# Hybrid RWKV-7 / sparse-attention block: two of a joint FFN tile's seven products made ahead, and the second merge begun with RWKV's part

## The chip, the cores and the metric

The kernel runs on one core of a Trainium2 chip. The metric is device time in microseconds (us), the median of a few runs. Beside the times there is one profiled execution, whose span is counted from its first to its last recorded instruction. Engines are named as in the profile: PE is TensorE, PEld its weight load, DVE VectorE, ACT ScalarE, POOL GpSimd, SP the engine that issues most DMAs.

## The reference

One decoder layer over 1024 tokens with model width 1024, in fp32:

```python
u = rmsnorm(x, norm1_g);  proj = u @ w_in
y_a = rwkv7_mix(token_shift(p_rwkv), ...)              # 8 heads of 64, a scan over tokens
y_b = dsa_attention(rope(q), rope(k), v, ...)          # 8 heads, 256 keys chosen per query
merged = sigmoid(p_ga) * (y_a @ w_o_rwkv) + sigmoid(p_gb) * (y_b @ w_o_att)
h = x + merged @ w_out
z_gate, z_up = split(rmsnorm(h, norm2_g) @ w_ffn_in)   # 2 x 2816 columns
h = h + (silu(z_gate) * z_up) @ w_ffn_out
out = rmsnorm(h, normf_g)
```

The change touches the second half of attention, the second merge, the FFN and the last norm.

## The kernel before

**Layout.** Activations lie transposed: 128 channels on the partitions, 512 tokens (one of two halves) along the free axis. A product over 1024 channels is eight blocks. Every fp32 product is made of three reduced-precision ones: an operand is split into a high part (an ACT copy into the fp32r type, line 114) and a low part (a DVE subtraction, line 115), and `mm3` multiplies high by high, high by low (lines 144 and 145) and low by high (149). A 128-column weight tile against one half thus costs 24 matmuls of 512 columns. `mm3_last` (159) and `mm3_late` (1232, 1236) are the same products in an order that needs the last block, or the low part of the activations, late.

**Weights.** `weights` loads a raw tile into one of three `wst` buffers (125) and splits it into `whi`/`wlo`, of which there are two pairs. PSUM has three accumulators `acc` and five `mix`; `tmp` is a ring of four scratch tiles, 512 wide.

**Order.** PE's order is written out by hand: it runs in program order. The other engines' orders are set by the framework's scheduler, with some blocks given a high priority, and each engine and DMA queue then serves in order. Work of the first half is laid into the gaps of other stages by generators: `fill` is a queue of them, each of which yields after a few matmuls with their number, and `pump(n)` advances the queue until n of them are spent. `run` exhausts a generator; `run_over` exhausts one, and spends the negative numbers that it yields on `fill`.

**The stages around the change.** During the RWKV scan of the second half, `fill` holds the last gate tile, the first half's merge and the first half's `early` FFN. Then `attend(1)` runs 16 units (four head pairs by four query blocks): scores, a masked minimum on DVE (1062), an exponent on ACT (1065), transposes (1074), values (1084), and at a head pair's end `close`, which sends the sums through DRAM and scales the output. Its yields say how much fill goes in between. After it the rest of the fill runs.

`merge(1)` loads y_a and y_b, splits them, makes both parts of `w_o` per 128 output columns under the two gates, then `w_out`, adds x, writes h to DRAM, makes the unnormalised z = h times the norm's gain, split into `zhi`/`zlo`, and sums the squares. The norm's factor per token (a row) is applied later, in `swiglu`, to the FFN's products. It is made in `columns` (sums over channels on PE, a power on POOL), then `spread` (259, 274).

The FFN has 22 tiles of 128 gate and 128 up columns. `early(half)` does tiles 0 to 7 and their output (`ffn_out`), then 8 to 11 and theirs, for one half. `joint` does tiles 12 to 21 for both halves: the 2 x 2 block product of [gate, up] weights (each cut into two channel halves) by the two token halves is made of seven products instead of eight, in the manner of Strassen and Winograd. Its combined activations `t1`, `t2`, `t3`, `t4` come from `combined` (POOL subtractions, then splits), the combined weights from POOL sums in `joint_in` (1404). `ffn_out` adds its result to h in DRAM. The last two tiles' output is made in `finish_out`, which keeps h in SBUF, and makes the last norm in three passes: the first half, then 256 and 256 tokens of the second.

## Time and profile before

| | us |
|---|---|
| median of 3 runs | 1789.42 |
| lowest, highest | 1788.69, 1790.65 |
| the profiled execution | 1789.51 |
| its span | 1787.7 |
| mean granted clock of PE | 0.982 |

A row of a group reads: line, engine, operation, output<-inputs by the program's names, shape, count; busy us, mean ns; idle time of the engine before them and what ended it. In a list in order of time, a bracket holds the idle time just before the instruction and what released it.

### The profile page before, as it was taken

The numbers are of one execution on the slowest core, as the hardware profiler recorded it, in microseconds if no ns is written. First come the engines' busy times: TensorE is split into PE (matmuls) and PEld (weight loads), VectorE is DVE, ScalarE is ACT, GpSimd is POOL, SyncE is SP. The second block draws the span as 40 slices with busy tenths as digits, with TensorE's granted clock in tenths as the row PEclk, the third lists the DMA queues.
The fourth block names the chain that finished last, engine by engine and source line by source line (L and its number), as shares of the span: only waits on it lengthen the run. The fifth ranks groups of instructions, "written<-read, shape, count | busy, mean of one in ns | idle before, by whom it ended". The sixth has DMA issues, their size and how long they took to land. (4 is left out here: it accounts for less than half of the span.)

```text
span 1787.7 us, 26739 instructions
## 1 busy us (share of the span) xinstructions
PE 1707.8 (96%) x9952; PEld 1397.8 (78%) x9952; DVE 1191.6 (67%) x2249; ACT 834.7 (47%) x1592; POOL 222.8 (12%) x203
## 2 busy tenths in 40 slices
PE   8999999999999989999999999798799989999996
PEld 6888888788877767887888887586688878888785
DVE  6789899865576468758857655456753558567467
ACT  6365997543444877544333547333331323123132
POOL 0000000010021110000002111005700032031030
PEclk9999999999999999999999999898999999999998
DMA  5542334444375336733345674463235351541633
GB/s 205 175 138 83 107 104 149 144 127 146 122 208 160 105 109 204 218 112 99 113 125 159 192 204 130 161 195 98 68 113 170 92 159 54 159 142 41 208 130 128
DMA packets 139874, 248.20 MB, mean 139 GB/s; under 512 B 37680, under 2 KB 61936, under 8 KB 139616
## 3 DMA queue, kind: packets, MB, share of 16 engines
q1 hardware_dynamic: 116384, 172.66, 31.0%
q10 hardware_dynamic: 15552, 47.75, 8.5%
q0 software_dynamic: 7808, 26.09, 5.4%
q8 instruction: 78, 1.28, 0.3%
q14 instruction: 52, 0.43, 0.1%
HBM read 185.06 MB, written 61.39 MB: 138 GB/s over the span
## 5 line engine op out<-in xcount | busy, mean ns | idle before, releaser
L115 DVE TENSOR_TENSOR wlo<-wst,whi 128x1024 fp32r<-128x1024 f32 (+1 forms) x209 | 240.5, 1152 | 179.3 <-PE acc L149 78.6
L114 ACT ACTIVATE whi<-wst 128x1024 fp32r<-128x1024 f32 (+1 forms) x209 | 202.4, 970 | 269.6 <-PE acc L145 167.1
L144 PE MATMUL acc<-zhi,whi 128*128 128x512 f32 x352 | 142.2, 404 | 12.6 <-ACT whi L114 5.7
L144 PE MATMUL acc<-u1hi,whi 128*128 128x512 f32 x352 | 140.9, 400 | 0.0
L145 PE MATMUL acc<-zlo,whi 128*128 128x512 f32 x352 | 140.1, 398 | 0.0
L145 PE MATMUL acc<-u1lo,whi 128*128 128x512 f32 x352 | 138.8, 394 | 0.0
L144 PE MATMUL acc<-u0hi,whi 128*128 128x512 f32 (+1 forms) x352 | 135.3, 387 | 1.8 <-DVE tmp L343 1.8
L145 PE MATMUL acc<-u0lo,whi 128*128 128x512 f32 (+1 forms) x352 | 133.8, 383 | 0.0
L144 PE MATMUL acc<-fhi,whi 128*128 128x512 f32 x256 | 101.8, 398 | 1.9 <-ACT whi L114 1.0
L145 PE MATMUL acc<-flo,whi 128*128 128x512 f32 x256 | 100.1, 391 | 0.0
L144 PEld LDWEIGHTS acc<-zhi,whi 128*128 128x128 f32 x352 | 68.0, 193 | 29.4 <-ACT whi L114 6.7
L149 PE MATMUL acc<-u1hi,wlo 128*128 128x512 f32 x352 | 90.3, 395 | 0.0
L149 PE MATMUL acc<-zhi,wlo 128*128 128x512 f32 x352 | 88.4, 391 | 0.0
L149 PE MATMUL acc<-u0hi,wlo 128*128 128x512 f32 (+1 forms) x352 | 86.6, 385 | 0.0
L144 PEld LDWEIGHTS acc<-u1hi,whi 128*128 128x128 f32 x352 | 67.4, 191 | 14.8 <-DVE tmp L334 0.5
L145 PEld LDWEIGHTS acc<-zlo,whi 128*128 128x128 f32 x352 | 68.1, 193 | 13.7
L144 PEld LDWEIGHTS acc<-u0hi,whi 128*128 128x128 f32 x352 | 66.2, 188 | 15.2 <-ACT stg L114 2.2
L145 PEld LDWEIGHTS acc<-u1lo,whi 128*128 128x128 f32 x352 | 67.3, 191 | 13.4
L149 PEld LDWEIGHTS acc<-u1hi,wlo 128*128 128x128 f32 x352 | 65.6, 189 | 14.3 <-issue 1.0
L149 PEld LDWEIGHTS acc<-zhi,wlo 128*128 128x128 f32 x352 | 65.6, 188 | 13.5
L145 PEld LDWEIGHTS acc<-u0lo,whi 128*128 128x128 f32 x352 | 66.2, 188 | 12.2
L149 PEld LDWEIGHTS acc<-u0hi,wlo 128*128 128x128 f32 x352 | 64.0, 188 | 13.1 <-issue 0.7
(403 smaller groups left out, 3948.0 us busy)
## 6 DMA issues: line engine op xcount, KB each, us to landing
wst<-in_w_ffn_in SPq DMA_DIRECT2D x52, 512.0 KB, 4.1
wst<-in_w_in ACTq DMA_DIRECT2D x36, 512.0 KB, 3.7
tmp<-d_h SPq DMA_DIRECT2D x64, 256.0 KB, 3.5
d_h<-tmp SPq DMA_DIRECT2D x64, 256.0 KB, 4.6
wst<-in_w_in SPq DMA_DIRECT2D x27, 512.0 KB, 3.8
k<-d_k POOLq DMA_DIRECT2D x24, 512.0 KB, 8.8
h<-in_xT SPq DMA_DIRECT2D x32, 256.0 KB, 5.2
d_g<-tmp ACTq DMA_DIRECT2D x32, 256.0 KB, 2.9
```

The lines of the kernel that those rows point to most:

```text
L114: A.activation(hi, x, AF.Copy)
L115: V.tensor_tensor(lo, x, hi.bitcast(F32), op=ALU.subtract)
L144: T.matmul(ps, whi[:, wk + k, :], ahi[:, ak + k, tok], start=k == 0, stop=False)
L145: T.matmul(ps, whi[:, wk + k, :], alo[:, ak + k, tok], start=False, stop=False)
L149: T.matmul(ps, wlo[:, wk + k, :], ahi[:, ak + k, tok], start=False, stop=k == nk - 1)
```

## The change

- `EARLY` is tiles 0 to 7 alone; `JOINT` is 8 to 11, 12 to 14, 15 to 17 and 18 to 21. So 14 tiles are joint, and `finish_out` has four tiles' output.
- Two of the seven products read the first half's tokens and uncombined gate weights alone. A new generator `ahead` makes them for one tile, scales them with the first half's row, and writes two results to DRAM (`d_p`): the first product p, and silu of the gate of the first half. Fourteen such generators are appended to `fill`. `joint_in` reads them into a ring and makes the other five products.
- `scaled` writes the first half's normalised z to DRAM (`d_z`), eight blocks during attention, on POOL; `combined` reads it from there.
- In `attend(1)` the yields fall from 5, 4, 4 to 2, 1, 1; `pump(130)` before it becomes `pump(106)`. A negative yield in `run_over` now means whole generators (`tiles`). The rest of the fill runs after `merge(1)`.
- `merge(1)` makes RWKV's part of w_o for all eight column blocks first and keeps it in `mid`, then attention's part. Its z is multiplied by the norm's row before it is split, so the products of the second half need no row afterwards. Three fill tiles are placed along the norm.
- `early(1)` uses the first half's pool for its activations; `ffn_out` of the joint blocks has a ring of eight tiles instead of `tmp`.

```diff
-EARLY = [(0, 8), (8, 4)]
-JOINT = [(12, 4), (16, 4), (20, 2)]
+EARLY = [(0, 8)]
+JOINT = [(8, 4), (12, 3), (15, 3), (18, 4)]
...
+    def tiles(n):
+        for _ in range(n):
+            if fill:
+                run(fill.popleft())
+        credit[0] = 0
...
         for n in gen:
             if n < 0:
-                pump(-n)
+                tiles(-n)
...
-    def merge(half, zp, zs):
+    def merge(half, zp, zs, jp=None):
...
-        yield -20
+        yield -2 if half else -20
+        if half:
+            mid = jp.tile([128, 8, HT], F32, tag="t3", name="mid")
+            for d in range(8):
+                w = weights(ins["w_o"][d][:, 0:4, :], 4)
+                ga = tmp()
+                SY.dma_start(ga, d_g[half][d])
+                pa = acc()
+                yield from mm3(pa, w, yt, nk=4)
+                V.scalar_tensor_tensor(mid[:, d, :], ga, 1.0, pa, op0=ALU.add, op1=ALU.mult)
         for j in range(4, 8):
             split(yhi[:, j, :], ylo[:, j, :], ylo[:, j, :].bitcast(F32))
...
+            if half:
+                w = weights(ins["w_o"][d][:, 4:8, :], 4)
+                gb = tmp()
+                SY.dma_start(gb, d_g[half][8 + d])
+                pb = acc()
+                yield from mm3(pb, w, yt, nk=4, ak=4)
+                ga = mid[:, d, :]
+                V.scalar_tensor_tensor(gb, gb, 1.0, pb, op0=ALU.add, op1=ALU.mult)
+                V.tensor_tensor(ga, ga, gb, op=ALU.add)
...
+        if half:
+            yield -1
+            sq.columns()
+            yield -1
+            row = sq.row(zp, "s2")
+            for d in range(8):
+                V.scalar_tensor_tensor(h[:, d, :], h[:, d, :], par[:, P_N2 + d:P_N2 + d + 1], row, op0=ALU.mult,
+                                       op1=ALU.mult)
+                A.activation(zhi[:, d, :], h[:, d, :], AF.Copy)
+            yield -1
+            for d in range(8):
+                V.tensor_tensor(zlo[:, d, :], h[:, d, :], zhi[:, d, :].bitcast(F32), op=ALU.subtract)
...
+    def swiglu(f, j, g, u):
+        t = tmp()
+        silu(t, g)
+        V.scalar_tensor_tensor(t, t, 0.5, u, op0=ALU.mult, op1=ALU.mult)
         split(f[0][:, j, :], f[1][:, j, :], t)
+    def ahead(j, zs):
+        (zhi, zlo), _, row = zs
+        w = weights(ins["w_ffn_in"][2 * j])
+        pss = [acc(), acc()]
+        for i, ps in enumerate(pss):
+            yield from mm3(ps, w, (zhi, zlo), nk=4, wk=4 * i, ak=4 * i)
+        p, x, t = tmp(), tmp(), tmp()
+        V.tensor_tensor(p, pss[0], row, op=ALU.mult)
+        SY.dma_start(d_p[j][:, 0, :], p)
+        V.tensor_tensor(x, pss[1], row, op=ALU.mult)
+        V.tensor_tensor(x, x, p, op=ALU.add)
+        silu(t, x)
+        SY.dma_start(d_p[j][:, 1, :], t)
+    def scaled(k, zs):
+        (zhi, zlo), _, row = zs
+        x = tmp()
+        G.tensor_tensor(x, f32(zhi[:, k, :]), f32(zlo[:, k, :]), op=ALU.add)
+        G.tensor_tensor(x, x, row, op=ALU.mult)
+        SY.dma_start(d_z[k], x)
...
+        pa, pb, pc, pd = acc(), mix(), mix(), mix()
+        mm(pa, wb, 0, "t2")
+        V.tensor_tensor(p1, p1, pa, op=ALU.add)
+        mm(pb, wb, 4, "t1")
+        V.tensor_tensor(w, p1, pb, op=ALU.add)
+        mm(pc, wc, 0, "t3")
+        V.tensor_tensor(c, w, pc, op=ALU.add)
+        mm(pd, wd, 0, "22")
+        V.tensor_tensor(w, w, pd, op=ALU.add)
+        swiglu(f, gn + i, w, c)
+        mm(pc, wc, 4, "t4", False)
+        V.tensor_tensor(p1, p1, pc, op=ALU.add)
+        V.scalar_tensor_tensor(t0, t0, 0.5, p1, op0=ALU.mult, op1=ALU.mult)
+        split(f[0][:, i, :], f[1][:, i, :], t0)
...
+        fill.extend(ahead(j, z0) for j in range(JOINT[0][0], NFF))
...
-        pump(130)
-        for n in attend(1, ap, bias):
+        pump(106)
+        for i, n in enumerate(attend(1, ap, bias)):
             pump(abs(n))
+            if i % 8 == 4 and i < 64:
+                scaled(i // 8, z0)
+    if fill:
+        tiles(1)
+    sb.close()
+    (sz1, zp1), z1 = opened("right", "zp1"), []
+    with tc.tile_pool(name="jp", bufs=1, side="right", reuse_waits="tile") as jp:
+        run_over(merge(1, zp1, z1, jp))
         run(*fill)
```

More of the change, by code (lines that the diff above doesn't have):

```diff
@@ L97, in block_kernel @@
     d_yb = scratch("d_yb", [4, 128, HT])
+    d_p = {j: dp.tile([128, 2, HT], F32, name=f"d_p{j}") for j in range(JOINT[0][0], NFF)}
+    d_z = dp.tile([8, 128, HT], F32, name="d_z")
     d_s = dp.tile([4, 2, HT], F32, name="d_s")
@@ L276, in spread, with row @@
             return rb[:, :128 * self.n]
-        def row(self):
+        def row(self, pool=tp, tag="sacc", **kw):
             rb = self.spread()
-            row = tp.tile([128, HT], F32, tag="sacc", name="row", bufs=2)
+            row = pool.tile([128, HT], F32, tag=tag, name="row", **kw)
             A.activation(row, rb, AF.Copy)
@@ L414, in scale @@
         def scale(half):
-            rows[half] = sqs[half].row()
+            rows[half] = sqs[half].row(bufs=2)
             for i in range(2):
@@ L1200, in merge @@
                                    op1=ALU.subtract)
-        yield -10
+        if half == 0:
+            yield -10
         h = zp.tile([128, 8, HT], F32, tag="s0", name="h")
@@ L1216, in merge @@
             V.tensor_tensor(h[:, d, :], h[:, d, :], ps, op=ALU.add)
-            A.activation(zhi[:, d, :], h[:, d, :], AF.Copy, scale=par[:, P_N2 + d:P_N2 + d + 1])
+            if half == 0:
+                A.activation(zhi[:, d, :], h[:, d, :], AF.Copy, scale=par[:, P_N2 + d:P_N2 + d + 1])
             SY.dma_start(d_h[half][d], h[:, d, :])
-            sq.add(d)
+            sq.add(d, last=half == 1 and d == 7)
+        if half:
[10 more added lines that the diff above has]
+                V.tensor_tensor(zlo[:, d, :], h[:, d, :], zhi[:, d, :].bitcast(F32), op=ALU.subtract)
+            zs.extend((zt, h))
+            return
         for d in range(8):
@@ L1249, in ffn_in @@
                     yield n
-                    if i == 3:
-                        sq.columns(smp.tile([128, 4], F32, name="rsz") if half == 0 else None)
-                zs.append(sq.row())
-                yield 4
+                    if i == 3 and half == 0:
+                        sq.columns()
+                if half == 0:
+                    zs.append(sq.row(bufs=2))
+                    yield 4
             else:
@@ L1277, in add @@
         def add(d, half, ps):
-            t = tmp()
+            t = tmp() if ring is None else ring[:, (2 * d + half) % 8, :]
             SY.dma_start(t, d_h[half][d])
@@ L1305, in norm_out, with finish_out @@
             SY.dma_start(outT[k * 128:(k + 1) * 128, half * HT + sq.tok.start:half * HT + sq.tok.stop], u)
-    def finish_out(zps, f, g0, gn):
-        whi, wlo = (zps[0].tile([128, 8, gn, 128], F32R, tag=t, name=n) for t, n in (("s0", "fhi"), ("s2", "flo")))
-        hs, ws, before = [], [], None
-        for zp in zps:
-            hs.append(zp.tile([128, 8, HT], F32, tag="s1", name="h"))
+    def finish_out(zps, jp, f, g0, gn):
+        whi, wlo = (zps[0].tile([128, 8, gn, 128], F32R, tag=t, name=n) for t, n in (("s1", "fhi"), ("s3", "flo")))
+        hs = [jp.tile([128, 8, HT], F32, tag="t3", name="h"), zps[1].tile([128, 8, HT], F32, tag="s1", name="h")]
+        ws, before = [], None
         for half in range(2):
@@ L1354, in early @@
             yield from ffn_in(half, f, zs, g0, gn)
-            if half and (g0, gn) == EARLY[-1]:
+            if (g0, gn) == EARLY[-1]:
                 yield 0
@@ L1360, in f32, with pool, combined @@
         return x.bitcast(F32)
-    def combined(zps, z0, z1, jp):
-        def pool(op, o, a, b):
-            G.tensor_tensor(o, f32(a), f32(b), op=op)
-        def recon(z, k):
-            t = jp.tile([128, HT], F32, tag="t", name="t", bufs=3)
-            pool(ALU.add, t, z[0][:, k, :], z[1][:, k, :])
-            return t
+    def pool(op, o, a, b):
+        G.tensor_tensor(o, a, b, op=op)
+    def combined(zps, z, h, jp):
+        t1, t2 = (zps[0].tile([128, 2, 4, HT], F32R, tag=t, name=n) for t, n in (("s1", "t1"), ("s3", "t2")))
+        t4 = zps[1].tile([128, 2, 4, HT], F32R, tag="s2", name="t4")
@@ L1406, in joint_in @@
+        bs["t3"], bs["22"] = (tuple(x[:, 4 * i:4 * i + 4, :] for x in z) for i in range(2))
+        yield bs
+    def joint_in(f, gn, i, j, bs, ring, jp):
+        p1, t0, w, c = (ring[:, j % 2, e, :] for e in range(4))
+        SY.dma_start(ring[:, j % 2, 0:2, :], d_p[j])
         with tc.high_priority():
             g, u = (raw_weights(ins["w_ffn_in"][2 * j + e]) for e in range(2))
-            wa, wb = ([wp.tile([128, 8, 128], F32R, tag=t, name=t) for t in ("whi", "wlo")] for _ in range(2))
+            wb = [wp.tile([128, 8, 128], F32R, tag=t, name=t) for t in ("whi", "wlo")]
```

133 lines of the change are left out of this document (49 added, 84 removed).

## The prediction, made before the change was run

> **What bounds the kernel now.** I read the page's first lines, then a table of busy time by stage, then PE's idle places.
>
> ```profile
> span 1787.7 us, 26739 instructions
> PE 1707.8 (96%) x9952; PEld 1397.8 (78%) x9952; DVE 1191.6 (67%) x2249; ACT 834.7 (47%) x1592; POOL 222.8 (12%) x203
> ```
>
> TensorE (PE) is busy for 96%, so the kernel costs its matmuls plus what PE loses between them: 1787.7 - 1707.8 = 79.9 us idle, and some more at half clock. I cut the part that the change touches where PE's operands change. Columns: stretch, its length, busy time of PE, weight load, DVE, ACT and POOL, granted clock, DMA share, GB/s.
>
> ```profile
> 969.00:999.20 30.20, 30.20 (x137) 25.01 (x136) 14.67 (x18) 8.71 (x12) 10.34 (x16) 1.00 0.91 263
> 999.20:1080.00 80.80, 80.80 (x548) 67.61 (x546) 45.23 (x111) 44.57 (x88) 14.83 (x28) 1.00 0.66 181
> 1080.00:1121.80 41.80, 38.12 (x396) 32.25 (x394) 19.91 (x58) 29.49 (x64) 2.78 (x3) 1.00 0.38 105
> 1121.80:1133.32 11.52, 0.27 (x3) 0.08 (x1) 0.71 (x2) 1.42 (x4) 0.00 (x0) 0.64 0.59 188
> ...
> 1133.32:1180.28 46.96, 46.74 (x193) 37.59 (x194) 31.86 (x44) 16.83 (x22) 0.00 (x0) 0.94 0.54 178
> 1180.28:1224.60 44.32, 44.09 (x193) 35.96 (x192) 21.03 (x26) 18.23 (x24) 0.21 (x1) 1.00 0.58 180
> 1224.60:1337.43 112.83, 97.66 (x401) 78.41 (x400) 76.28 (x75) 34.42 (x46) 56.97 (x35) 0.92 0.26 83
> 1337.43:1381.77 44.34, 43.82 (x194) 35.97 (x192) 15.96 (x18) 9.01 (x9) 0.00 (x0) 1.00 0.58 174
> 1381.77:1425.29 43.52, 43.52 (x194) 36.05 (x192) 21.37 (x27) 12.99 (x17) 0.00 (x0) 1.00 0.33 92
> 1425.29:1454.62 29.33, 24.08 (x97) 19.11 (x96) 16.90 (x22) 6.74 (x11) 9.43 (x6) 0.88 0.60 185
> 1454.62:1533.65 79.03, 78.21 (x346) 63.66 (x344) 56.71 (x75) 25.76 (x39) 22.23 (x16) 1.00 0.21 61
> 1533.65:1577.82 44.17, 44.10 (x193) 35.89 (x192) 20.22 (x30) 7.71 (x11) 4.00 (x4) 1.00 0.71 224
> 1577.82:1654.80 76.98, 76.65 (x337) 62.92 (x336) 55.68 (x75) 24.44 (x37) 17.79 (x13) 1.00 0.20 63
> 1654.80:1700.17 45.37, 44.39 (x193) 35.81 (x192) 20.23 (x30) 7.70 (x11) 3.62 (x3) 1.00 0.72 215
> 1700.17:1738.53 38.36, 38.36 (x169) 31.45 (x168) 24.94 (x41) 12.63 (x23) 11.01 (x14) 1.00 0.29 92
> 1738.53:1787.70 49.17, 32.93 (x181) 28.72 (x179) 36.63 (x80) 13.14 (x27) 6.77 (x11) 0.82 0.41 153
> ```
>
> The stages: attention of the second half with leftover work of the first half as fill (to 1080) and without (to 1121.8); a dead wait; the second merge (w_o, then w_out); the second half's early FFN (eight tiles in, out, four in, out); three joint blocks with two outputs between; the finish. The undisturbed stage, 1381.77 to 1425.29, gives the price of a 512-column matmul: 43.52/192 = 0.2267 us. Half-width ones I count as half. Against that price each stage's loss follows from the kernel's loop counts: attention 3.7, wait 11.5, w_o 3.4 (192 matmuls, 43.5), w_out 0.8, ffn_in 25.7 (384, 87.1), ffn_out 0.8, second ffn_out 7.6 (96, 21.8), joint blocks and outputs 2.8, 0.6, 0.8, 1.8 and 0.3, finish 27.4 (96, 21.8). Together 87.2 us: all that better cover could win.
>
> ```profile
> 1121.80 0.27 PE L1104 MATMUL mix<-kc,ri 128*8 128x128 f32 x1
> 1133.32 0.80 PE L144 MATMUL acc<-yhi,whi 128*128 128x512 f32 x1 [11.25 <-ACT yhi L114]
> ...
> 1434.86 0.80 PE L159 MATMUL acc<-fhi,whi 128*128 128x512 f32 x1 [5.25 <-ACT fhi L114]
> 1435.45 0.63 PE L159 MATMUL acc<-fhi,wlo 128*128 128x512 f32 x1
> 1435.88 0.63 PE L159 MATMUL acc<-flo,whi 128*128 128x512 f32 x1
> ```
>
> ```profile
> PE acc L159 <- ACT fhi L114: 5.3, 1, 5.3
> PE acc L144 <- DVE tmp L1266: 5.0, 1, 5.0
> PE mix L1074 <- DVE mx L1062: 3.1, 1, 3.1
> ```
>
> PE has nothing from attention's last matmul to the merge's first, then waits for the output's last tile (5.3) and for slow SwiGLU in the stretch where POOL is busy for half (5.0). After a long gap matmuls start 0.43 us apart (1435.45, 1435.88) where 0.23 is usual.
>
> **The change part by part.** *Matmuls.* A full tile costs 96 (two products, two halves, 24 each), a joint one 7 x 12 = 84. Four tiles (8 to 11) become joint: -48, or -10.9 us. FFN-out stays at 1056. Of 84, the 24 of the two first-half products move to `ahead`, 14 x 24 = 336; a joint tile keeps 60, or 13.6 us.
>
> *The fill's ledger.* From 969 before spends 130 credits, then 186 fill matmuls by 1080 (my count of the timeline between 999.2 and 1080): 316 were left. After: 316 - 288 (four tiles in and out) + 336 = 364. Spent: 106 ahead of attention; 112 by its yields (32 logits at 2, 32 turns and 16 values at 1); 18 in closing. 128 remain, 5.3 tiles: the rest of one, two at the merge's start, three along the norm. It comes out even, with nothing over. Up to 969 nothing changes.
>
> *Attention.* Fill merely moves work where PE is full (80.80 of 80.80). Spread to the end it covers the 3.7. Added are 16 POOL operations (`scaled`) and 0.5 MB stores per tile into a stretch whose DMA share is 0.91: about 3.3 tiles, 1.7 MB, at 263/0.91 = 289 GB/s some 6 us of DMA, against 2.7 free. The POOL operations stand ahead of later q, k and v issues on POOL's queue; those loads run a head pair ahead. I take a loss of 4.5; ends 1 (prefetch absorbs it) and 10 (all late).
>
> *Merge start.* RWKV's w_o part needs no attention output.
>
> ```profile
> 1128.94 1.88 SPq L1178 DMA_DIRECT2D ylo<-d_ya  x4
> ```
>
> Its loads stand on SP behind attention's last store, so y still arrives some 11 us after attention's last matmul. Cover: a third of a tile and two tiles, 56 x 0.2267 = 12.7 us, besides the fill in closing. Then 96 matmuls, 21.8 us, cover y_b. The 11.5 and the cold 3.4 go; without the cover they return as 14.9. Next late: the second w_o part has per column block on DVE a split, two products' steps and the low half, 4 x 0.69 = 2.75, against PE's 12 x 0.2267 = 2.72: level. Loss 2 (0 to 4).
>
> ```profile
> L1280 DVE TENSOR_TENSOR tmp<-tmp,acc 128x512 f32<-128x512 f32 x33 | 22.3, 682 | 21.0 <-PE acc L149 13.7 <-DMA tmp<-d_h 7.3
> L115 DVE TENSOR_TENSOR wlo<-wst,whi 128x512 fp32r<-128x512 f32 x26 | 18.0, 691 | 27.4 <-PE acc L149 20.9 <-PE acc L1430 4.5 <-PE mix L1430 1.9
> ...
> L115 DVE TENSOR_TENSOR wclo<-wst,wchi 128x1024 fp32r<-128x1024 f32 x10 | 12.3, 1233 | 13.6 <-ACT wchi L114 13.6
> ...
> L1265 DVE SCALAR_TENSOR_TENSOR tmp<-tmp,t 128x512 f32<-128x512 f32 x9 | 9.4, 1048 | 0.0
> ...
> L1265 DVE SCALAR_TENSOR_TENSOR tmp<-tmp 128x512 f32<-128x512 f32 x10 | 6.9, 686 | 0.5 <-ACT tmp L1264 0.5
> ```
>
> *Norm before FFN.* The second half's z is now scaled before its splits: an added wait on PE, which has the whole early FFN behind it. Chain from w_out's end: one tile (5.4), column sums (1), a tile (5.4) beside DVE and POOL, spread and row (1.3), then eight DVE products at 0.69 and the last ACT copy, taken as long as one (6.2): with DVE's other work zhi is whole at about 20. PE has work to 18.1 and can start the first group on early blocks. Loss, with the small matmuls, 3. Ends: 1.6 (no gap), 8 (DVE first finishes the fill tiles' 3.9 us each).
>
> *Early FFN.* Of 40 POOL operations 16 remain here, and SwiGLU drops from five DVE operations to three. DVE per tile: 2.4 (splits) + 2.0 + 2.0 (three combined splits) = 6.4 of 10.9. The 25.7 shrinks to 3 (0 to 10). The second output and its 7.6 vanish; the first keeps 0.8.
>
> *Joint tile.* DVE before: splits 4.1, sums 3.4, two SwiGLUs 6.6 = 14.1 of 19.05, and the table's 55.68/4 = 13.9 agrees. After: splits 3.0, sums 3.4, one SwiGLU 2.0, one shortened 1.3 = 9.7 of 13.6: 71% against 73%. So PE stays the bound; I take 0.4 lost per tile, 5.6 in all (before: 5 in ten, norm row included).
>
> ```profile
> L1404 POOL TENSOR_TENSOR wst<-wst 128x512 f32<-128x512 f32 x20 | 28.0, 1399 | 1.6
> ```
> ```profile
> wst<-in_w_ffn_in SPq DMA_DIRECT2D x52, 512.0 KB, 4.1
> ...
> k<-d_k POOLq DMA_DIRECT2D x24, 512.0 KB, 8.8
> ```
>
> Its weights: there are three raw buffers, and a tile's second load waits for the split of the tile before that frees one, about 2 before that tile begins; 4.1 of load, three POOL operations (4.2), a split (0.7) make 9, against 13.6 + 2: 6 us spare. With the 8.8 that attention's loads take, 2 would be left. The stored products wait on SP for a ring slot two tiles old, free long before. Three outputs (192, 144, 144) at 1.0 lost: 3.
>
> The row at 1048 beside that at 686 is the same operation, with two operands in SBUF and beside POOL; it bounds what POOL's share of 5.6 in 13.6 can do. The Trainium skill's "SBUF — State Buffer", section "Who interferes with whom", speaks against this edit: a DVE instruction with two SBUF inputs and a GpSimd one that reads SBUF take a shared port as an exclusive lock, so one waits for the whole of the other. The 1048 against 686 agrees with it; how far it adds up is the first rival.
>
> *Finish.* Four tiles instead of two: 192 for 96, +21.8 of PE work moved here from an output stage.
>
> ```profile
> 1774.89 0.40 PE L149 MATMUL acc<-fhi,flo 128*128 128x256 f32 x2
> ...
> 1776.66 0.83 PE L259 MATMUL mix<-kc,sacc 128*128 128x2 f32 x4 [1.38 <-DVE sacc L251]
> ...
> 1780.70 3.22 DVE L1304 SCALAR_TENSOR_TENSOR h<-h,par,mix 128x256 f32<-128x256 f32 x8 [2.16 <-PE mix L274]
> ```
>
> From the last wide matmul (1775.3) to 1787.7 is 12.4 of norm and store: it stays. The remaining 15 of the 27.4 are DVE-bound: two sums cost DVE 1.37 per block, PE 6 x 0.2267 = 1.36 before and 2.72 after, so PE now covers them. Left: one gap of 1.8 where eight norm products (8 x 0.69 and 0.4 to start) outlast the three accumulators that PE has free (three half-width blocks, 4.1), small matmuls 2.5, cold clock 0.7. Loss 17.4 (16 to 20).
>
> *Sum.* Losses after: 4.5 + 2 + 0.8 + 3 + 3 + 0.8 + 5.6 + 3 + 17.4 = 40.1. Span: 1787.7 - 10.9 - (87.2 - 40.1) = 1729.7. The profiled execution took 1789.5, 1.8 beside its span (median shown 1789.4), so **1732 us**.
>
> **The rivals.** *DVE and POOL add up in the joint tile.* For: the 1048 ns row. Against: before, 14.1 + 5.6 = 19.7 would exceed the 19.25 measured per tile, and sums that read PSUM stay at 682. Fully serial, 9.7 + 5.6 = 15.3, 1.3 over 13.6 + 0.4: 14 x 1.3 = 18, so 1750. The lock of the Trainium skill's SBUF page, named above, would give that upper end.
>
> *The cover does not cover.* The change then does not do what it says: the ledger has no spare tile, and if fill is spent in attention, the y wait (14.9) or an uncovered norm of 12 stands open: 1744 to 1759. For: the even ledger; against: counts are exact to a few matmuls.
>
> *Thin fill makes attention's chain the bound (slower than before).*
>
> ```profile
> 1088.29 0.27 PE L1104 MATMUL mix<-kc,ri 128*8 128x128 f32 x1
> ...
> 1111.20 0.27 PE L1104 MATMUL mix<-kc,ri 128*8 128x128 f32 x1
> ```
>
> Each unit (scores, minimum, exponent, turn, values) has 7 fill matmuls where it had 22. If DVE and POOL make the chain longer than a unit's PE work, every unit gets the 3.1 gap above and, if it grows past what chills the clock, some 2 us of half clock (ten matmuls at 0.43 for 0.23): 16 x 5.1 = 82, so 1814. It decides from a chain of about 6.5 us per unit (the four units between these two rows, without fill, took 5.7 each with that gap in one of them, 0.8 on the mean; plus 7 fill matmuls, 1.6). Against: without any fill PE was busy for 38.12 of 41.80, with one such gap.
>
> **How the numbers follow.** Forecast (1714 to 1744) 0.68; first rival, up to 1765, 0.15; second 0.10; third 0.04; below 1714 0.03. All terms at their best ends lose 23: 1715. Several bad ends together with the first rival lead to about 1765. Range 1714 to 1765. A measurement of this kernel tells 0.2%, 3.6 us, from no change; apart from the third rival a few chances in a hundred hold mishaps that eat 55 us: faster 0.93, same 0.02, slower 0.05.
>
> **What would show it.** Right: about 48 fewer wide matmuls; no gap over 3 us between attention and w_o; joint tiles every 14 us; a finish of about 61. Wrong: joint tiles of 15 us or more with DVE above 90%; PE waiting for zhi after the second w_out by more than 5 us; gaps in every attention unit. The prediction falls most easily if DVE in the early FFN and joint tiles is later than its busy time says, since it serves in order.

## The result, and the profile after

The changed kernel took **1767.2 us** (median of 4 runs, 1764.2 to 1771.2) where the kernel before took 1789.1 on the same chip: a ratio of 0.988, 95% interval 0.986 to 0.990. It is faster by 22 us; 57 were forecast, and the time lies 2 us above the range. The profiled execution took 1764.2 us, with this first part of its page:

```profile
span 1762.4 us, 26864 instructions
...
PE 1690.7 (96%) x9952; PEld 1386.7 (79%) x9952; DVE 1175.9 (67%) x2253; ACT 824.5 (47%) x1585; POOL 233.5 (13%) x211
```

TensorE (PE) is still busy for 96%. Its busy time is 17.1 us shorter (a matmul at a lower clock counts as busy for longer, so this is more than the 10.9 forecast for the matmuls), and the span is 25.3 shorter. The number of matmuls is the same only because the finish does work worth 48 full-width products as 96 of half width: counted at full width 48 are gone, as forecast. The table of busy time by stage, cut where PE's operands change (columns as in the prediction: stretch, length, PE, weight load, DVE, ACT, POOL, granted clock, DMA share, GB/s):

```profile
969.00:1080.00 111.00, 105.10 (x750) 87.70 (x749) 63.90 (x148) 61.91 (x123) 47.48 (x62) 0.98 0.79 225
1080.00:1122.28 42.28, 42.28 (x314) 35.68 (x313) 24.65 (x49) 21.35 (x43) 0.00 (x0) 1.00 0.30 106
1122.28:1170.94 48.66, 45.87 (x193) 36.94 (x192) 34.30 (x54) 18.38 (x30) 0.00 (x0) 0.96 0.75 239
1170.94:1216.22 45.28, 44.08 (x193) 35.97 (x192) 21.16 (x26) 14.58 (x18) 0.00 (x0) 1.00 0.67 212
1216.22:1235.32 19.10, 19.10 (x98) 16.20 (x96) 12.67 (x20) 5.88 (x9) 2.70 (x2) 1.00 0.46 145
1235.32:1333.54 98.22, 90.79 (x385) 72.94 (x384) 57.29 (x67) 37.70 (x53) 29.42 (x15) 0.98 0.39 118
1333.54:1377.88 44.34, 43.82 (x194) 35.97 (x192) 19.59 (x24) 11.21 (x15) 6.57 (x5) 1.00 0.65 208
1377.88:1435.05 57.17, 54.99 (x241) 44.90 (x240) 37.91 (x51) 16.04 (x24) 16.11 (x12) 1.00 0.30 97
1435.05:1481.10 46.05, 43.84 (x194) 35.97 (x192) 19.84 (x30) 7.79 (x12) 7.60 (x6) 1.00 0.66 212
1481.10:1523.44 42.34, 41.10 (x182) 33.71 (x180) 27.02 (x37) 10.97 (x17) 9.67 (x7) 1.00 0.37 122
1523.44:1561.14 37.70, 33.37 (x145) 26.71 (x144) 18.61 (x30) 7.15 (x12) 6.67 (x5) 1.00 0.75 240
1561.14:1605.48 44.34, 42.83 (x181) 34.97 (x181) 27.09 (x38) 11.08 (x17) 10.83 (x8) 0.96 0.39 128
1605.48:1643.35 37.87, 33.38 (x145) 26.72 (x144) 18.59 (x30) 7.14 (x12) 6.65 (x5) 1.00 0.71 232
1643.35:1701.82 58.47, 56.71 (x240) 46.12 (x241) 41.04 (x55) 18.56 (x28) 23.38 (x25) 0.97 0.42 138
1701.82:1762.40 60.58, 49.70 (x325) 45.23 (x323) 38.86 (x80) 13.86 (x28) 4.64 (x7) 0.95 0.29 106
```

The dead wait of 11.5 us between attention and merge is gone: matmuls run up to 1122.28 (42.28 of 42.28) and w_o begins there. Against the same price of 0.2267 us per matmul, each stage loses:

| stage | measured | forecast |
|---|---|---|
| attention, up to w_o | 8.6 | 4.5 |
| w_o and w_out | 6.9 | 2.8 |
| norm and early FFN-in (456 matmuls, 103.4, in 117.3) | 14.0 | 6 |
| early FFN-out | 0.8 | 0.8 |
| joint tiles (54.4, 40.8, 40.8, 54.4 without loss) | 11.9 | 5.6 |
| three outputs (43.5, 32.6, 32.6 without loss) | 12.8 | 3 |
| finish | 17.1 | 17.4 |
| sum | 72.1 | 40.1 |

The 32.0 us between the sums are nearly all of the 32.7 by which the span missed its forecast of 1729.7. Half of them, 16.1, lie in the joint tiles and their outputs, 8.0 in the norm and early FFN-in. The waits of PE behind w_o's start (what waited, for what: us in total, times, longest):

```profile
PE acc L1495 <- DVE more L1361: 8.6, 2, 4.4
PE mix L1495 <- DVE ring L1507: 6.7, 6, 1.5
PE acc L146 <- ACT whi L116: 6.1, 3, 3.5
PE acc L146 <- DVE mid L1199: 2.4, 1, 2.4
PE acc L146 <- DVE more L1361: 2.2, 1, 2.2
```

(`more` is the output's ring, whose adds read an accumulator bank of PSUM and so free it; `ring` holds a joint tile's sums; `whi` is a weight's high part; `mid` is RWKV's part of w_o.) The sum has a term for each stage, but names none of these five waits. Two look like a slow DVE, yet DVE is busy for 61 to 70% of the joint stages (27.09 of 44.34, 41.04 of 58.47). What it does ahead of the longest, in DVE's own order (start, us, operation, in brackets the idle time ahead of it and what ended that):

```profile
1550.84 0.69 DVE L1361 TENSOR_TENSOR more<-more,acc 128x512 f32<-128x512 f32 x1 [0.83 <-PE acc L151]
1555.35 1.33 DVE L117 TENSOR_TENSOR wclo<-wst,wchi 128x1024 fp32r<-128x1024 f32 x1 [3.82 <-ACT wchi L116]
1558.50 0.69 DVE L117 TENSOR_TENSOR wdlo<-wst,wdhi 128x512 fp32r<-128x512 f32 x1 [1.82 <-ACT wdhi L116]
1559.11 0.69 DVE L117 TENSOR_TENSOR wlo<-wst,whi 128x512 fp32r<-128x512 f32 x1
1559.71 0.69 DVE L117 TENSOR_TENSOR wlo<-s,whi 128x512 fp32r<-128x512 f32 x1
1560.32 1.88 DVE L1361 TENSOR_TENSOR more<-more,acc 128x512 f32<-128x512 f32 x3
```

```profile
1561.14 0.47 PE L1495 MATMUL acc<-t,whi 128*128 128x512 f32 x1 [4.22 <-DVE more L1361]
...
1562.48 0.63 PE L1495 MATMUL acc<-t,whi 128*128 128x512 f32 x1
1562.91 0.63 PE L1497 MATMUL acc<-t,whi 128*128 128x512 f32 x1
```

PE was done with the output at 1556.92 and only needed an accumulator bank back. The last three adds, 0.6 us each, could have given it, but they stand behind four splits of the next tile's weights, and DVE sat idle for 3.82 and 1.82 us in front of two of these. Idle and late at once: that speaks for an order, not a load. Behind the wait matmuls start 0.43 us apart (1562.48, 1562.91) instead of 0.23. The Trainium skill's "PSUM — Partial Sum Buffer", section "Engine vs sequencer instructions", has the queues of ScalarE, VectorE and GpSimd as strict first in, first out; these rows agree.

The splits are late because POOL, which makes what they split, is:

```profile
1551.57 1.28 POOL L1443 TENSOR_TENSOR s<-wst 128x512 f32<-128x512 f32 x1 [48.86 <-DVE more L1361]
...
1555.68 2.13 POOL L1443 TENSOR_TENSOR wst<-wst 128x512 f32<-128x512 f32 x1
```

Its first sum needs the tile's second raw block. In the chain that ended last this stands ahead of it (start, us, what):

```profile
1544.78 0.57 DVE wlo L117
...
1545.37 6.07 DMA wst<-in_w_ffn_in
```

The split at 1544.78 is one of the output's weights and gives a raw buffer back; only then was the block's load issued, and it landed at 1551.44, after 6.07 us where the prediction had 4.1. (POOL's row names a DVE add that ended just then, at 1551.53.) Edit 6 below gives the block a place of its own.

The 3.5 us wait for whi in the early FFN is the same thing on ACT. First ACT's rows, then POOL's, then DVE's:

```profile
1250.07 0.63 ACT L116 ACTIVATE t<-h 128x512 fp32r<-128x512 f32 x1 [7.24 <-POOL h L1443]
1251.41 0.63 ACT L116 ACTIVATE t<-t 128x512 fp32r<-128x512 f32 x1 [0.71 <-POOL t L1443]
1251.95 1.04 ACT L116 ACTIVATE whi<-wst 128x1024 fp32r<-128x1024 f32 x1
```

```profile
1241.82 6.86 POOL L1443 TENSOR_TENSOR h<-h 128x512 f32<-128x512 f32 x1 [7.77 <-DVE zlo L1265]
```

```profile
1243.84 3.09 DVE L1265 TENSOR_TENSOR zlo<-h,zhi 128x512 fp32r<-128x512 f32 x5
```

The weights that PE waits for stand on ACT behind splits of the combined activations (`put`), which wait for POOL; and POOL's subtraction took 6.86 us, five times its usual length, while DVE ran two-operand work in SBUF. The delay begins there, with POOL slowed beside DVE, and ACT's queue hands it on to PE.

### The profile page after: what moved, and what is told of

Read it like the earlier page. It is cut to its first block, busy times and chain, and to the rows that moved or that the text cites. A ratio compares the mean times of both kernels' runs of the same rounds, so it can differ in the third digit from the quotient of the medians.

```text
span 1762.4 us, 26864 instructions
## 1 busy us (share of the span) xinstructions
PE 1690.7 (96%) x9952; PEld 1386.7 (79%) x9952; DVE 1175.9 (67%) x2253; ACT 824.5 (47%) x1585; POOL 233.5 (13%) x211
## 4 chain that ended last, share of the span: by engine, by line
PE 67%; DVE 12%; ACT 7%; DMA 6%; issue 4%; POOL 4%; SPq 0%; POOLq 0%; DVEq 0%; ACTq 0%
PE acc L146 14%; PE acc L147 14%; PE acc L151 14%; PE acc L161 3%; PE mix L1495 2%; PE mix L1499 2%; PE mix L1497 2%; DVE wlo L117 2%; PE mix L934 2%; DMA wst<-in_w_ffn_in 2%; PE mix L1093 2%; ACT junk L984 2%; ACT junkl L984 1%; PE mix L1069 1%; POOL wst L1443 1%
## 5 line engine op out<-in xcount | busy, mean ns | idle before, releaser
L117 DVE TENSOR_TENSOR wlo<-wst,whi 128x1024 fp32r<-128x1024 f32 (+2 forms) x201 | 224.2, 1117 | 179.4 <-ACT whi L116 80.4
L116 ACT ACTIVATE whi<-wst 128x1024 fp32r<-128x1024 f32 (+2 forms) x201 | 186.9, 932 | 266.6 <-PE acc L147 194.0
L146 PE MATMUL acc<-zhi,whi 128*128 128x512 f32 x336 | 134.5, 400 | 8.9 <-ACT whi L116 5.6
L146 PE MATMUL acc<-u0hi,whi 128*128 128x512 f32 (+1 forms) x352 | 135.3, 387 | 1.7 <-DVE tmp L352 1.7
L147 PE MATMUL acc<-zlo,whi 128*128 128x512 f32 x336 | 132.6, 395 | 0.0
L146 PE MATMUL acc<-fhi,whi 128*128 128x512 f32 x236 | 92.9, 394 | 3.2 <-DVE more L1361 2.2
L147 PE MATMUL acc<-flo,whi 128*128 128x512 f32 x236 | 91.9, 389 | 0.0
L146 PEld LDWEIGHTS acc<-zhi,whi 128*128 128x128 f32 x336 | 64.0, 190 | 24.5 <-ACT whi L116 6.7
L147 PEld LDWEIGHTS acc<-u1lo,whi 128*128 128x128 f32 x352 | 67.1, 191 | 13.3
L147 PEld LDWEIGHTS acc<-zlo,whi 128*128 128x128 f32 x336 | 64.0, 191 | 12.6
```

The costliest lines, as they stand in the source:

```text
L116: A.activation(hi, x, AF.Copy)
L117: V.tensor_tensor(lo, x, hi.bitcast(F32), op=ALU.subtract)
L146: T.matmul(ps, whi[:, wk + k, :], ahi[:, ak + k, tok], start=k == 0, stop=False)
L147: T.matmul(ps, whi[:, wk + k, :], alo[:, ak + k, tok], start=False, stop=False)
```

## The experiments

Two theories. **Queue order**: DVE and ACT have the time, but serve in order, and an instruction that waits (for a load, a buffer or another engine) holds up one that PE needs. **Shared load** (the prediction's first rival): POOL and DVE slow each other in SBUF, so that DVE is truly too slow. Ratios are to the kernel before on the same chip; "from w_o" is the profiled span less the start of w_o, so without the stages ahead, which vary from run to run (last section).

| run | median us | ratio [95%] | from w_o |
|---|---|---|---|
| the changed kernel, first runs | 1767.2 | 0.988 [0.986, 0.990] | 640.1 |
| the changed kernel again | 1769.6 | 0.988 [0.985, 0.992] | 645.8 |
| 1 `put` splits later | 1764.1 | 0.985 [0.982, 0.989] | 638.5 |
| 2 output adds first | 1773.6 | 0.991 [0.988, 0.994] | 648.6 |
| 3 gates early | 1769.8 | 0.990 [0.988, 0.992] | 642.6 |
| 4 own bank | 1771.3 | 0.990 [0.988, 0.992] | 644.6 |
| 6 buffers for first tile | 1770.9 | 0.989 [0.985, 0.993] | 642.4 |
| 2 + 4 | 1768.3 | 0.987 [0.985, 0.989] | 642.7 |
| 1 + 2 + 3 + 4 | 1757.2 | 0.983 [0.980, 0.985] | 629.3 |
| 1 to 5 | 1754.2 | 0.978 [0.975, 0.981] | 628.5 |
| 1, 3, 4, 5, 6 | 1746.2 | 0.977 [0.974, 0.980] | 621.2 |
| **1 to 6** | **1745.4** | **0.975 [0.973, 0.977]** | **619.9** |
| all but 4 | 1761.1 | 0.983 [0.981, 0.985] | 635.0 |
| all but 5 | 1756.1 | 0.979 [0.977, 0.982] | 631.3 |
| all but 1 | 1751.2 | 0.977 [0.976, 0.979] | 627.7 |
| POOL's extra work, unplaced | 1772.0 | 0.990 [0.988, 0.992] | 645.7 |
| POOL's extra work, held in the joint tile | 1781.5 | 0.996 [0.994, 0.998] | 666.1 |
| fill spent in attention | 1785.7 | 0.998 [0.996, 1.001] | (fill moved) |
| second merge in one pass | 1774.0 | 0.990 [0.987, 0.992] | 647.6 |

The first two rows are the same kernel, and their last column differs by 5.7 us: by itself a difference of that size there tells nothing.

**The control.** The changed kernel unchanged.

> The changed kernel itself, for the same chip as the three below. Queue order (the theory: DVE and ACT serve in order, and an operation that would free PE stands behind one that waits for POOL or a DMA) and shared load (the prediction's first rival: DVE and POOL together are too slow) expect the same: 1764 to 1771 us, with waits of about 2, 4 and 4 us behind the three joint outputs.

It came out 2.4 us slower than at first, within its own spread of some 10 us; differences of single edits are read with that in mind.

**Edit 1, the combined activations' splits behind the SwiGLU's.**

```diff
         def put(t, k, x):
-            split(t[:, 0, k, :], t[:, 1, k, :], x)
+            with tc.issue_after(done[0].ins), tc.issue_after(done[1].ins):
+                split(t[:, 0, k, :], t[:, 1, k, :], x)
```
(`done` holds the two instructions of the last SwiGLU split; `issue_after` fixes the order on the engine.)

> In the second half's early FFN the splits of the combined activations are held behind the SwiGLU of the tile before, on ACT and DVE, so that no weight split stands behind one that waits for POOL. Queue order: the waits of 3.5 and 2.1 us for weight splits in that stage go, with 1.7 of half clock: 5 to 7 us faster than the changed kernel. Shared load: POOL and DVE do the same work, within 2 us.

The norm and the early FFN-in took 111.0 us instead of the control's 118.7, and no wait for whi was left there. In the time it gained about 5 us, with intervals that overlap.

**Edit 2, the output's adds ahead of the next tile's splits.**

```diff
-            split(wb[0][:, 0:4], wb[1][:, 0:4], g1)
+            with tc.issue_after(last_add[0].ins) if i == 0 else nullcontext():
+                split(wb[0][:, 0:4], wb[1][:, 0:4], g1)
...
```

> The first joint tile of a block may not have its low-part splits on DVE ahead of the last sum of the output before. Nothing else changes. Queue order: the waits of 2.2, 4.2 and 4.4 us behind the outputs fall under 1 each, with the half clock after two of them (1.7 each): 8 to 13 us faster than the changed kernel. Shared load: as many operations as before, so within 2 us of it.

A miss, and not faster. Its waits:

```profile
PE mix L1498 <- DVE ring L1510: 15.8, 8, 3.4
...
PE acc L1498 <- ACT whi L116: 4.2, 2, 2.6
```

The adds' wait is gone (8.6 in the profile after, 11.5 in the control's), but the joint tile's bank wait grew from 6.7 to 15.8 and the new tile now waits 4.2 for its own splits. The wait had moved.

**Edit 4, a bank of its own for the fourth product of a joint tile.** The product `t4` accumulates onto `pc`, which DVE must have read first; the prediction never priced that wait.

```diff
-        mm(pc, wc, 4, "t4", False)
+        pe = acc()
         V.tensor_tensor(p1, p1, pc, op=ALU.add)
+        mm(pe, wc, 4, "t4")
+        V.tensor_tensor(p1, p1, pe, op=ALU.add)
```

> The fifth product of a joint tile goes to a bank of its own instead of being added onto the third product's bank, which DVE still has to read; DVE gets one more sum per tile (0.68 us). If the wait for that read is what joint tiles lose: the six waits (6.7 us, and some 0.4 more each) go, 6 to 9 us faster than the changed kernel. Shared load: 14 more sums on an engine that is the bound, 5 to 10 us slower.

The bank waits vanished and undisturbed joint tiles took 13.6 us, the bare price. The time moved neither way (2 us slower by the medians, 3 by the ratios), so both expectations missed. PE then waited elsewhere:

```profile
PE acc L1495 <- DVE more L1361: 10.8, 2, 6.4
PE acc L161 <- DVE ring L1514: 6.7, 1, 6.7
```

The adds' wait stayed (11.5 in the control), and one of 6.7 appeared ahead of the finish: as much as the bank waits had been.

**Edit 3, the gates early.** `d_g` is loaded straight into `mid`, ahead of the fill, and not through a `tmp` buffer.

```diff
+            for d in range(8):
+                SY.dma_start(mid[:, d, :], d_g[half][d])
+        yield -2 if half else -20
...
-                ga = tmp()
-                SY.dma_start(ga, d_g[half][d])
```

> The gates of the second merge's RWKV half are loaded straight into the tile that keeps its partial sums, ahead of the first stretch of fill, so that no temporary buffer has to come free for them. In the profile after, the first VectorE product of that merge (L1199) makes TensorE wait 2.40 us at 1133.86, and the two microseconds behind it run at half clock. Queue order (a wait for a buffer held by stores stands at the head): that wait and the slow clock behind it go, about 4 us less than the changed kernel, 1763 to 1766 beside a control of 1767 to 1770. Shared load (VectorE and GpSimd slow each other by their shared port): nothing in this place, within 1 us of the control.

In its place it did what it should:

```profile
1128.79:1173.50 44.71, 44.32 (x194) 35.88 (x192) 34.26 (x54) 18.69 (x31) 0.00 (x0) 1.00 0.81 260
```

The pass takes 44.7 us at full clock where it took 48.7 at 0.96 (46.9 in the control). By the whole time the gain can't be told: at 1769.8 us it missed the 1763 to 1766 of queue order, and what it gains is smaller than the spread.

**Edits 1 to 4 together, and 2 with 4.**

> All four edits together: combined products' splits behind the SwiGLU's, the first joint tile's splits behind the last output add, a bank of its own for the fourth product of a joint tile, and the gates early. Queue order: each of the second and the third alone only moved its wait to the place that the other one removes, so together they save what alone they gave back: the 6.7 us of bank waits, the 8 to 13 us behind the outputs, the 5 us that the first edit showed, the 4 us of the gates; less one VectorE sum for each of 14 tiles and a wait of up to 6 us at the start of the finish: 1748 to 1756. Shared load: no less than the first edit alone, 1762 to 1770, because VectorE's and GpSimd's work is the same or more.

> The two edits that alone gave nothing, together: a joint group's first splits stand behind the last output add, and the fourth product of each joint tile has a bank of its own. Queue order: the adds no longer wait behind splits, and the splits' lateness no longer reaches a bank wait, so the waits behind the outputs shrink from 12 to about 4 us and the bank waits (6.7 us in the profile after, 15 us with the first edit alone) go; 14 more VectorE sums and a wait of about 7 us at the finish stay: 5 to 10 us less than the control of 1769.6, 1760 to 1765. If the two waits are not the same lateness seen in two places, the pair is worth what they were alone, nothing or less: 1770 to 1775.

All four gave 1757, 12 us less than the control by the medians and 10 by the ratios, 1 above what queue order expected and below the other theory's 1762. The pair alone gave no gain that can be told, a miss: its bank waits were gone, but 8.1 us stood ahead of the finish.

**Edit 5, the finish's weight splits.** The splits of the finish's last five weight blocks stand on ACT, waiting for their loads, ahead of the tanh of the last SwiGLU.

```diff
                 st = raw_weights(ins["w_fo"][d][:, g0:g0 + gn, :], gn)
-                split(whi[:, d], wlo[:, d], st)
+                if d < 3:
+                    split(whi[:, d], wlo[:, d], st)
+                else:
+                    with tc.issue_after(last_f[0].ins), tc.issue_after(last_f[1].ins):
+                        split(whi[:, d], wlo[:, d], st)
```

> The four edits and a fifth: of the finish's eight weight tiles the splits of the last five stand behind the last joint tile's own split, so that the tanh of the last SwiGLU and VectorE's last sums no longer stand behind splits that wait for their weights from memory. In the profile with the four edits TensorE waits 7.54 us at 1693.99 for a VectorE sum (L1520) that ends 8 us after its matmul, with ScalarE idle in front of five such splits. Queue order: that wait shrinks to about 2 us, 5 to 6 us less than the 1757.2 of the four edits, 1750 to 1753. If the wait has another cause, or the later splits make the finish's own products wait, no gain: 1755 to 1760.

The 7.5 us wait went, but the waits for a group's first joint tile's splits grew from 3.0 to 8.1 us together, and the gain (3 us by the medians, 8 by the ratios, 0.8 from w_o) can't be told from the spread: moved again. That says that the splits themselves were late, which no order mends; edit 6 tests it.

**Edit 6, buffers for the first tile.** The first tile of a joint group loads one raw block into two small tiles that lie idle there, so that POOL need not wait for a raw buffer of the output.

```diff
-            g, u = (raw_weights(ins["w_ffn_in"][2 * j + e]) for e in range(2))
+            g = raw_weights(ins["w_ffn_in"][2 * j])
+            if i == 0:
+                us = [jp.tile([128, 4, 128], F32, tag="t", name="u0", bufs=2) for _ in range(2)]
+                for e in range(2):
+                    SY.dma_start(us[e], ins["w_ffn_in"][2 * j + 1][:, 4 * e:4 * e + 4, :])
...
```

> One edit on the changed kernel: the first tile of each joint group loads one of its two raw weight blocks into two small tiles that lie idle there, in place of a raw buffer that the output stage still holds. Its GpSimd chain and its splits then come some 4 us earlier and stand between the output adds instead of ahead of the last three. If late raw buffers are what makes the adds wait, the waits of 2.2, 4.2 and 4.4 us behind the outputs shrink to under 1.5 each and the half clock behind two of them goes: 8 to 11 us less than the control of 1769.6, 1758 to 1762. If only the order on VectorE matters and not when the splits are ready, the waits stay or move into the joint tiles: 1766 to 1773.

> The edits of the best run but the one that holds the first splits behind the last add, and in its place buffers of their own for half of the first tile's raw weights. Late raw buffers: the three waits behind the outputs (2.1, 2.3 and 3.7 us in the best run's profile, with half clock behind the last) go: 5 to 9 us less than the 1754.2 of the best run, 1745 to 1750. Otherwise as the best run or worse: 1753 to 1760.

> All edits of the best run, the splits held behind the last add included, and buffers of their own for half of the first tile's raw weights. Holding ready splits back then costs what it saves: 1748 to 1754, between the best run and the run without the hold; if the hold matters and the buffers do not, 1752 to 1757, as the best run.

Alone it is a miss of the first expectation. The splits do come earlier (the first begins 9.6 us ahead of the next group's first matmul, at 1558.27 for 1567.85, where it was 5.8), and PE no longer waits at a group's first matmul; it waits instead inside the outputs (5.1) and for the bank (10.3). With the others it brings another 5 to 9 us. The run with all six came out below both of its expectations, so the hold behind the adds costs nothing that can be told. It is the fastest, 1745.4 us, faster than the changed kernel by about 24 and than the kernel before by 44 (2.5%). Its four joint stages:

```profile
1365.83:1420.58 54.75, 54.71 (x241) 44.97 (x240) 47.19 (x58) 15.07 (x23) 20.17 (x13) 1.00 0.31 102
...
1465.52:1506.32 40.80, 40.80 (x181) 33.78 (x180) 35.32 (x44) 11.14 (x18) 14.20 (x9) 1.00 0.45 141
...
1543.28:1584.08 40.80, 40.80 (x181) 33.78 (x180) 35.32 (x44) 11.13 (x18) 14.29 (x9) 1.00 0.46 160
...
1620.79:1676.51 55.72, 54.74 (x242) 44.93 (x240) 44.90 (x58) 15.59 (x24) 24.02 (x25) 1.00 0.39 126
```

Two of them run without any loss at all (40.80 of 40.80), while DVE is busier than ever, 35.32 of 40.80, 87%. A DVE that is too slow for 13.6 us could not do that. In the run without the hold (1, 3, 4, 5, 6) the joint tiles run at the bare price too, at a DVE share near that of the profile after:

```profile
1366.68:1421.08 54.40, 54.40 (x241) 45.06 (x240) 39.82 (x53) 15.11 (x24) 15.52 (x11) 1.00 0.28 85
1467.64:1508.44 40.80, 40.80 (x181) 33.79 (x180) 28.43 (x40) 11.37 (x18) 11.55 (x9) 1.00 0.42 128
```

DVE is busy for 73 and 70% there, and nothing is lost: the joint tiles' loss was one of order and buffers. Part of the 87% is slower splits (`wlo<-s` takes 1213 ns on the mean with the hold and 924 without), and PE loses nothing by that.

**One edit taken out of the six.**

> The best run without the bank of its own for the fourth product of a joint tile. If the joint tile's order is what all lateness ends in, the bank waits come back, 7 to 15 us as in the runs that kept it, and the 14 extra sums (9.5 us of VectorE, most of it beside TensorE) go: 5 to 14 us slower than the 1745.4 of the best run, 1750 to 1760. If the other edits made VectorE early enough, VectorE's sum is there in time and nothing is lost: 1743 to 1748.

> The best run without the hold of the finish's last five weight splits. In the run of four edits that stood for a wait of 7.54 us ahead of the finish; if it does so still, 1750 to 1754. If that wait came from lateness that the first-tile buffers took away, 1743 to 1748.

> The best run without the hold of the combined products' splits behind the SwiGLU's in the early FFN. That stage stands before all the others that were edited, and its loss was 5 to 6 us alone: 4 to 7 us slower, 1749 to 1753; the edit's worth does not hang on the others.

By the ratios' differences from 0.975, at 17.9 us for each hundredth, the edits are worth with the rest in place: the bank 14 us, the finish's order 8, the first-tile buffers 6 (0.978 against 0.975), the `put` order 5, the hold behind the adds 4. Only the bank's worth is clear of the intervals; the others' overlap. From w_o the same five are 15, 11, 9, 8 and 1 us, so that the finish's order, the buffers and the `put` order count there too, and the hold is not shown to. Edit 3 was not taken out. Apart from the hold's, the wait that came back was each edit's own: 7.6 us ahead of the finish, 8.1 for the first tiles' splits, 3.9 for whi in the early FFN, and without its bank:

```profile
PE mix L1516 <- DVE ring L1528: 14.4, 9, 3.6
```

Alone, edits 1, 2, 3, 4 and 6 had moved the time by -5, +4, +3, +3 and +1 us, by the ratios as well: no gain in sum, where the six together are worth 24.

**POOL's work in the joint tile doubled.** Two sums on a tile that nobody else reads are added for each of 14 tiles.

```diff
             pool(ALU.subtract, g2, g2, g1)
+            for _ in range(2):
+                pool(ALU.add, idle, idle, idle)
```

> Two more GpSimd sums for each of the 14 joint tiles, on a tile of their own that nobody reads, issued behind the chain that makes the combined activations: GpSimd's own time in a joint tile about doubles, nothing waits for it in this tile. Shared load: VectorE's two-operand work of a tile is held by what GpSimd adds, about 2.6 us for each tile, some 25 to 36 us slower than the control, 1793 to 1805, and TensorE's waits in every joint tile name VectorE. Queue order: VectorE is 64 to 70 per cent busy there, so most of it is absorbed; only the next tile's combined activations come later, up to 6 us in all, 1768 to 1776.

> As in the run with GpSimd's work doubled, but each pair of extra GpSimd sums is held directly behind the chain of its own joint tile (that run's 28 sums all stood between 1076 and 1109 us, in the attention, so it said nothing of the joint tiles). Shared load: a sum took 1.04 us, so 2.1 us more of GpSimd per tile; if VectorE's two-operand work waits for all of it, 14 x 2.1 = 29 us slower than the control, 1796 to 1802, or at least half of that, and joint tiles of about 16 us. Queue order: VectorE has 30 per cent of slack in these stages and absorbs most; joint tiles stay within 0.5 us of 14.4, the next chain is late at the first tiles alone, 0 to 6 us, 1769 to 1776.

The first told nothing of the joint tile: with nothing to wait for, all 28 sums ran between 1076 and 1109 us, in the attention, where nobody minded. The second holds each pair behind its own tile's chain. One of its joint stages, and the same stage of the control:

```profile
1494.30:1539.62 45.32, 42.99 (x182) 35.06 (x180) 28.95 (x37) 10.74 (x17) 13.15 (x10) 0.96 0.29 96
```

```profile
1486.06:1528.46 42.40, 41.16 (x182) 33.76 (x180) 26.99 (x37) 10.97 (x17) 8.02 (x6) 1.00 0.35 113
```

Over the four stages POOL was busy for 27.5 us more (85.8 for 58.3), DVE for 7.4 more (142.6 for 135.3), and the stages took 13.3 longer (216.8 for 203.6); in the time, 12 us by the medians, 14 by the ratios. (The profiled execution was the slowest of its ten, 11 us above their median, so the stages show rather too much.) DVE's work grew where it splits weights, with both operands in SBUF (control first):

```profile
L117 DVE TENSOR_TENSOR wlo<-s,whi 128x512 fp32r<-128x512 f32 x14 | 13.7, 978 | 3.4 <-ACT whi L116 3.4
```

```profile
L117 DVE TENSOR_TENSOR wlo<-s,whi 128x512 fp32r<-128x512 f32 x14 | 15.4, 1098 | 5.5 <-ACT whi L116 5.5
```

Both theories missed: 12 to 14 lies above 0 to 6, and just under half of the 29 of a full sum. So POOL does slow DVE, by a quarter of its own added time here, and the stages lose nearly twice that: the bank waits rose from 6.8 to 14.6 us. The Trainium skill's "SBUF — State Buffer", section "Who interferes with whom", has the two exclude each other for a whole instruction; the lengthened splits agree, but over the four stages DVE's busy time grew by only 7.4 us for POOL's 27.5. How much of the lost time POOL's own work causes was not tried; the run with all six edits has all of that work and loses nothing by it in two of its stages.

**Fill spent in attention.** The yields of the kernel before (5, 4, 4) and its pump of 130.

```diff
-                    yield 2 if half else (bi + 3) // 2
+                    yield 5 if half else (bi + 3) // 2
...
-        pump(106)
+        pump(130)
```

> The shares of fill in the second attention are those of the kernel before (5, 4 and 4 for 2 or 1) and the reserve pump is 130 for 106, so that the products made ahead are used up in the attention and nothing is left for the wait between attention and merge and for the norm. If the reserved fill is worth what the prediction took, the wait of 11.5 us and its half clock, the norm's stretch of 13 us and part of the early FFN come back: 15 to 27 us slower than the control, 1784 to 1796, with a gap of over 8 us ahead of w_o. If the attention covers those stretches by itself or its own waits shrink by as much, within 5 us of the control.

The dead wait is back, and all but 3 us of the change's gain is gone with it, 16 us in all by the medians:

```profile
1154.62 0.80 PE L146 MATMUL acc<-yhi,whi 128*128 128x512 f32 x1 [10.38 <-ACT yhi L116]
```

**The second merge in one pass.** The pass of RWKV's half ahead is taken out and w_o runs as before, behind the reserved fill.

```diff
-        if half:
-            mid = jp.tile([128, 8, HT], F32, tag="t3", name="mid")
-            for d in range(8):
-                w = weights(ins["w_o"][d][:, 0:4, :], 4)
...
```

> The change with the second merge's w_o in one pass, as the kernel before has it: each of eight outputs takes its RWKV half and its attention half in one go, and the reserved fill stands ahead of it alone. If the split in two passes is what covers the wait for the attention's last unit, part of the 11.5 us and its half clock come back: 6 to 14 us slower than the control, 1775 to 1784. If the fill reserved for that place covers the wait by itself, the 2.40 us wait for the gates and its half clock go and nothing comes in its place: 1764 to 1768.

Between both expectations: 4 us above the control by the medians, 3 by the ratios, within the noise. A wait of 1.7 us for yhi and a slower w_o (50.1 us) came, and the 2.4 us for the gates went. Of the cover for the 11.5 us, nearly all is the reserved fill; RWKV's part first is worth a few us at most.

## Why the prediction was wrong, point by point

- **Matmuls, -10.9:** right; 48 wide ones are gone.
- **The ledger and the merge's start:** right in mechanism. The 11.5 and its half clock are gone, and the run that spends the fill early brings them back at 16 us. The second rival (the cover does not cover) fell. The loss at w_o, 2 (0 to 4), was 5.1: the wait for gates in a shared buffer wasn't seen. Edit 3 takes it away.
- **Attention, 4.5 (1 to 10):** 8.6, inside the ends by luck. The term was for late loads of q, k and v, and PE waited 0.93 us for one of these; 2.88 us is one wait for a DVE sum (`ahead`, L1336) whose temporary buffer was still held by a store, 1.62 one for ACT. No run took that apart.
- **Thin fill (third rival):** fell. From 1080 to w_o PE is busy throughout.
- **Norm:** right; PE waits 1.7 us for zhi in all. **Early FFN, 3 (0 to 10):** with the norm 14.0 for 6. The prediction added up DVE's busy time per tile (6.4 of 10.9); the loss was on ACT's queue, behind `put`, which waited for POOL. Edit 1 took out 7.7 us of that stage and left 7.6.
- **Joint tiles, 0.4 each, and outputs, 1.0 each: the step that failed.** It read "71% against 73%" as "PE stays the bound". The load was about right (9.5 us of DVE per tile in the profile after for 9.7 forecast), and in the fastest run PE is the bound, at 13.6 us a tile in two of its stages. But DVE stood idle in front of splits with work behind them that PE needed, and 24.7 us were lost for 8.6 forecast. Two things were missing. "6 us spare" for the raw weights was worked out for a tile that follows a tile; behind an output the three buffers hold the output's weights, and the load took 6.07 us for 4.1. And `t4` waits for DVE to read `pc`, 6.7 us in six places, which the diff shows and the sum left out. None of the three signs that the prediction gave for being wrong appeared (tiles of 15 us with DVE above 90%, over 5 us for zhi, a gap in every unit): they look at load or at other places, and this was order.
- **First rival (DVE and POOL add up):** half true. The run with more POOL work shows that they do disturb each other, but by a quarter, and the stages without loss, at 70% and at 87% DVE, show that it isn't the bound.
- **Finish, 17.4:** right, 17.1; the gap of 1.8 was 1.9. The tail behind the last wide matmul took 10.8 us where 12.4 were to stay, and the rest of the stage made up for it.
- The last sentence of the prediction named the cause (DVE "later than its busy time says, since it serves in order"), and gave it no price. With all six edits the losses from w_o on are 43.3 (619.9 less 576.6; 63.5 in the profile after) for the 35.6 forecast. The sum comes nearer, in part because errors cancel: the joint tiles lose 1.7 for 5.6, the outputs 9.8 for 3, the finish 20.9 for 17.4.

What stays open: the waits in the attention, the finish, which is 3.8 us longer in the fastest run than in the profile after, and 9.8 us at the outputs of the fastest run, where PE still waits 4.7 for the adds.

## What to carry to other kernels

Busy shares tell whether an engine has the time, not whether it has it in time: where an engine that serves in order gets work of two stages, list for each boundary what stands ahead of the instruction that the bound engine needs, and what that in turn waits for, down to the buffer. An edit to such a chain may show nothing alone, because the lateness is met again at the next wait; look for where the wait went before giving the edit up, and test it by taking it out of the full set. And mind an accumulator that another engine must read before the next product may go in.

## What the runs showed of the hardware

- **The same work ahead of w_o took different times.** In the profiled runs w_o begins anywhere from 1121.0 to 1130.6 us, in kernels with the same attention, though edits other than 3 change nothing ahead of it. Between the run of 2 + 4 (w_o at 1121.1) and that of 1 to 5 (at 1130.6) the difference arises between about 480 us, where the same matmul starts 1.0 apart in the two, and 790, where one starts 10.2 apart. From 600 to 700 us the first had the full clock and the second did not:

```profile
600.00:700.00 100.00, 92.12 (x766) 72.10 (x764) 67.24 (x133) 83.25 (x197) 9.86 (x6) 1.00 0.43 133
```

```profile
600.00:700.00 100.00, 92.77 (x756) 73.03 (x756) 60.36 (x123) 80.11 (x190) 8.36 (x6) 0.93 0.36 114
```

  Why it falls one way or the other was not tried.
- **How long a wait slows the clock is not fixed.** After the 2.40 us wait at 1133.86 the granted clock was 0.59 from 1136 to 1139; after a wait of 2.49 us in the fastest run (at 1539.1) it stayed at 1.00. The Trainium skill's "TensorE: Matmul & The Clock Gate", "Part 1: The HAM clock gate (the "warmup" mystery)", puts the drop behind an idle window of some 3.4 us that runs freely; the variation agrees with a free-running window, the 2.40 does not agree with its length.
